# Norm scales broadcast by TensorE, two first output tiles that follow the input, and a last product whose split weights serve both token halves, in a two-layer hybrid trunk

## The chip, the cores and the metric

The kernel runs on one core of a Trainium2 chip. The metric is the device time of one execution in microseconds (us); smaller is better. Three executions of the kernel before the change took 1350.98 to 1352.93 us, with a median of 1351.63 us. One execution was also profiled.

## The reference: what is computed

The input is 512 tokens of 1024 channels in float32. Two layers add to it in place, each followed by a gated feed-forward part, and a norm ends it:

```python
def rms_norm(x, w, eps=NORM_EPS):
    y = x * lax.rsqrt(jnp.mean(x * x, axis=-1, keepdims=True) + eps)
    return y * w
...
x = x + pool_attention_mixer(rms_norm(x, norm_mix[0]), ...)   # pooling + windowed attention
x = x + conv_ffn(rms_norm(x, norm_ffn[0]), ...)
x = x + ssd_mixer(rms_norm(x, norm_mix[1]), ...)              # Mamba-2, with a norm of its own
x = x + conv_ffn(rms_norm(x, norm_ffn[1]), ...)
return rms_norm(x, norm_final)
...
def conv_ffn(h, w_up, conv_w, conv_b, w_down):
    hid = causal_dwconv(h @ w_up, conv_w, conv_b)             # 1024 -> 2 x 2816
    u, g = jnp.split(hid, 2, axis=-1)
    return (jax.nn.silu(g) * u) @ w_down                      # 2816 -> 1024
```

So there are six norms. Each needs, for every token, one number over all 1024 (in the Mamba part 2048) channels: the reciprocal root of a mean square.

## The kernel before

**Layout.** Channels lie on the 128 partitions and tokens along the free dimension, so `x` is eight tiles of 128 x 512. A product takes weights of 128 x 128 as the stationary operand and 512 tokens as the moving one. Each float32 operand is split into a high and a low part of type float32r, and `gemm` (L143 to L148) issues three matmuls for each pair: high by high (L146), high by low (L147), low by high (L148). Weights come in tiles of 128 x 1024 by DMAs on SyncE's queue (SP); ScalarE (ACT) rounds the high part (L138) and VectorE (DVE) subtracts it for the low part (L139). The buffers `w`, `wh` and `wl` have three copies each.

**A norm.** The norm's weights are multiplied into the activations when they are split (L151, L152). The scale of each token is applied only behind the next product, since it is the same for all channels: `scaled` (L232) multiplies the product in PSUM by `rb`, the 512 scales repeated on all 128 partitions. `Stat` makes them. ACT squares each tile of `x` (L171), GpSimd (POOL) adds the squares up (L172), TensorE sums over partitions with a column of ones (L179), and a chain of seven small operations (L183 to L189) makes a reciprocal root `rt` with tokens on the partitions (128 x 4). To lie along the free dimension on all partitions, `rt` goes by one DMA to `flat` in DRAM (L192) and by a second one back from there to `rb`, repeated 128 times (L194). Both are in SP's queue, in order with the loads of weights. The product does not wait for the scale, but its results stay in PSUM until `rb` is there, and PSUM has four buffers `mm`.

**The places by time** (us in the profiled execution): the first projection and pooling mixer (0 to 165, the attention in it from 74 on), the first feed-forward part (165 to 515), the Mamba part (515 to 990; it applies its `rb` at L232 for the projections, and that of its inner norm at L226, behind the product with `ssm_w_out`), and the second feed-forward part (990 to the end). The step sizes of the Mamba part (`sd`, L527) need `rt` itself, not `rb`.

**The start.** One output tile's weights, t0, are loaded behind the first tile of `x`; its products follow the input tile by tile. The tiles t1 and t2 follow as whole products. Two matmuls on constant data (`WARMUP`) stand ahead of them.

**The end.** `finish_out` (L242 to L262) does the last third of the last down product in two halves of 256 tokens, so that the output of the first half is written while the second is multiplied. Each half loads and splits the same eight weight tiles. The scale of the first half goes through `flat` and `rb`; that of the second half is broadcast by TensorE into PSUM (L198), `rt` repeated as the stationary operand by a unit matrix. Then DVE multiplies each tile by weight and scale (L260) and SP writes it (L262).

**The order of the work** on each engine is not the order of the source. A scheduler sorts the instructions by a simulated timeline ahead of time; each engine then runs its list in order and waits where an operand is missing.

Of the kernel before, what the change touches and what calls it, by code (L numbers as in the profile page):

```python
# [20 lines left out]
P = 128  # L21
T = 512
# [33 lines left out]
K_ROT = K_PH + 3  # L56
NCON = K_ROT + P

WARMUP = 2
INV2PI = 1.0 / (2.0 * math.pi)  # L60
MAGIC = 12582912.0
PI_C1 = 6.28125
# [6 lines left out]
def trunk_kernel(ctx: ExitStack, tc: tile.TileContext, io):  # L69
# [19 lines left out]
    def ct(dt=F32):  # L89
        return sp.tile([P, T], dt, tag="C", name=nm("c"), bufs=16)  # L90
# [4 lines left out]
    def t2(tag, bufs, dt=F32):  # L95
        return tp.tile([P, T], dt, tag=tag, name=nm(tag), bufs=bufs)
# [16 lines left out]
    nc.sync.dma_start(x[:, 0, :], io["xT"][:, 0, :])  # L113

    idle = t2("sq", 2)
    G.memset(idle[:], 1.0)
    A.activation(idle[:, 0:1], idle[:, 1:2], AF.Copy)
# [8 lines left out]
    def pc(c):  # L126
        return par[:, c : c + 1]


    def load_split(src, kt=8, cols=P, eng=None):  # L130
# [3 lines left out]
        nc.sync.dma_start(w[:, :kt, :cols], src)  # L134
        if eng is V:
            V.tensor_copy(h[:, :kt, :cols], w[:, :kt, :cols])
        else:
            A.activation(h[:, :kt, :cols], w[:, :kt, :cols], AF.Copy)  # L138
        V.tensor_tensor(out=l[:, :kt, :cols], in0=w[:, :kt, :cols],  # L139
                        in1=h[:, :kt, :cols].bitcast(F32), op=ALU.subtract)  # L140
        return h, l

    def gemm(ps, ws, kt, rh, rl, first=True, last=True, ts=slice(0, T)):  # L143
        h, l = ws
        for k in range(kt):
            PE.matmul(ps, lhsT=h[:, k, :], rhs=rh[k][:, ts], start=first and k == 0, stop=False)  # L146
            PE.matmul(ps, lhsT=h[:, k, :], rhs=rl[k][:, ts], start=False, stop=False)  # L147
            PE.matmul(ps, lhsT=l[:, k, :], rhs=rh[k][:, ts], start=False, stop=last and k == kt - 1)  # L148
# [7 lines left out]
    class Stat:  # L156
# [17 lines left out]
        def finish(self, dim, eps, copy=True):  # L174
# [14 lines left out]
            V.tensor_tensor(out=r, in0=r, in1=q, op=ALU.mult)  # L189
            if copy:  # L190
                flat = dp.tile([NB, P], F32, tag="flat", name=nm("flat"), bufs=2)
                nc.sync.dma_start(flat[:nb, :].rearrange("c p -> p c"), r)  # L192
                rb = t2("rb", 1)
                nc.sync.dma_start(rb[:, :w], flat[:nb, :].rearrange("c p -> (c p)").partition_broadcast(P))  # L194
                return rb, r
            pb = aux()
            for c in range(nb):
                PE.matmul(pb[:, c * P : (c + 1) * P], lhsT=r[:, c : c + 1].to_broadcast([P, P]), rhs=ident,  # L198
# [43 lines left out]
    def finish_out(down, nj, kh, kl):  # L242
        H = T // 2
        warm = tp.tile([P, 1], F32, tag="warm", name="warm", bufs=1)
        A.activation(warm[:], ones[:, 0:1], AF.Sqrt)
        scale = []
        for half in range(2):
            ts = slice(half * H, (half + 1) * H)
            stat = Stat(KD, H, late=2)
            for n in range(KD):  # L250
                ws = load_split(down[n], nj)
                ps = mm()
                gemm(ps[:, :H], ws, nj, kh, kl, ts=ts)
                V.tensor_tensor(out=x[:, n, ts], in0=ps[:, :H], in1=x[:, n, ts], op=ALU.add)
                stat.add(x[:, n, ts])
            scale.append(stat.finish(D, EPS, copy=half == 0)[0])
        for half in range(2):
            ts = slice(half * H, (half + 1) * H)
            for k in range(KD):
                V.scalar_tensor_tensor(out=x[:, k, ts], in0=x[:, k, ts], scalar=pc(C_NFIN + k),  # L260
                                       in1=scale[half][:, :H], op0=ALU.mult, op1=ALU.mult)
                nc.sync.dma_start(io["out"][k * P : (k + 1) * P, ts], x[:, k, ts])  # L262


    def ffn(layer, cur, nxt):
# [68 lines left out]
        return res  # L334


    def mixer(cur, nxt, first_ws):
        poolw = tp.tile([P, 4, P], F32, tag="R", name="poolw", bufs=3)
        nc.sync.dma_start(poolw[:], io["poolw"])
        rb, rt = cur.stat.finish(D, EPS)  # L340
        hp, lp, ha, la = bt(), bt(), bt(), bt()

        def project(t):
            ws = first_ws[t] if t < len(first_ws) else load_split(io["wmi"][t])
            ps = mm()
            gemm(ps[:], ws, KD, cur.hs, cur.ls)
            return ps


# [396 lines left out]
```

## Time and profile before

| | |
|---|---|
| median of three runs | 1351.63 us (1350.98 to 1352.93) |
| the profiled execution's own time | 1350.57 us |
| its span, from the first to the last instruction | 1348.8 us |
| TensorE busy (modelled ends) | 1294.2 us, 96% |
| DVE, ACT, POOL busy | 877.4, 594.7 and 183.8 us |
| share of the chain that ended last | PE 83%, DMA 7%, DVE 4%, ACT 2%, issue 2%, POOL 1% |
| mean granted clock of TensorE | 0.986 |

A row of the timeline reads: start, length (both us), engine, line, operation, output and inputs, and in brackets how long the engine had been idle before and on what. In a row of waits stand the waiting engine and line, what it waited for, the total, the number of times and the longest. A row of windows has, behind the stretch and its length, the busy time and the number of instructions of PE, of its weight loads (PEld), of DVE, ACT and POOL, then the mean granted clock, the share of the DMA engines in use and GB/s.

### The profile page before, as it was taken

To read this page: it belongs to the slowest core of one execution; us is meant where nothing else is said; L and a number is where in the kernel's file an instruction comes from. 1 tells how busy PE (TensorE), PEld (TensorE's weight loads), DVE (VectorE), ACT (ScalarE), POOL (GpSimd) and SP (SyncE) were. 2 spreads that over 40 slices of the span, in tenths; PEclk is the share of its full clock that TensorE was granted. 3 is DMA by queue.
4 is the path that set the end of the run, shared out by engine and by line. 5 is a ranking of instruction groups with operands and counts; after the bars stand their busy time and mean duration, and the time that the engine had idled before them with its cause. 6 is when DMAs were issued, how large, how long until landed. Compare 5 with 4: busy or idle time off the path is not lost.

```text
span 1348.8 us, 16284 instructions
## 1 busy us (share of the span) xinstructions
PE 1294.2 (96%) x6242; PEld 1055.9 (78%) x6242; DVE 877.4 (65%) x1348; ACT 594.7 (44%) x813; POOL 183.8 (14%) x167
## 2 busy tenths in 40 slices
PE   7898999999999999899999999988999999999995
PEld 5665878888888887778888888777878888888895
DVE  6664568457647764687888878844577467557764
ACT  6273445234324444465556655532344234324451
POOL 4552300000000012021222122212000000000021
PEclk9989999999999999999999999998999999999998
DMA  6411233333233323343333333213233332333352
GB/s 231 135 33 47 94 86 102 102 103 97 78 114 96 101 89 95 91 122 109 100 105 105 114 95 105 84 63 89 91 97 92 105 105 88 99 96 106 97 157 82
DMA packets 46574, 134.81 MB, mean 100 GB/s; under 512 B 8288, under 2 KB 10720, under 8 KB 46496
## 3 DMA queue, kind: packets, MB, share of 16 engines
q1 hardware_dynamic: 45856, 132.46, 31.9%
q0 software_dynamic: 640, 1.31, 0.4%
q8 instruction: 49, 0.80, 0.2%
q14 instruction: 29, 0.24, 0.1%
HBM read 129.74 MB, written 2.17 MB: 98 GB/s over the span
## 4 chain that ended last, share of the span: by engine, by line
PE 83%; DMA 7%; DVE 4%; ACT 2%; issue 2%; POOL 1%; SPq 0%; DVEq 0%; ACTq 0%; POOLq 0%
PE mm L146 26%; PE mm L148 26%; PE mm L147 25%; DMA flat<-rt 3%; DMA rb<-flat 2%; PE yp L621 1%; DVE wl L139 1%; PE yp L624 1%; DMA R<-scr 1%; ACT wh L138 1%; PE ax L627 1%; PE mm L412 1%; PE yp L447 1%; DVE c L238 1%; PE ax L451 1%
## 5 line engine op out<-in xcount | busy, mean ns | idle before, releaser
L146 PE MATMUL mm<-a,wh 128*128 128x512 f32 x1232 | 485.3, 394 | 13.0 <-DVE p L226 7.5
L147 PE MATMUL mm<-a,wh 128*128 128x512 f32 x1232 | 484.3, 393 | 5.3 <-DVE a L152 5.3
L148 PE MATMUL mm<-a,wl 128*128 128x512 f32 x1232 | 485.6, 394 | 2.3 <-DVE wl L139 2.3
L138 ACT ACTIVATE wh<-w 128x1024 fp32r<-128x1024 f32 (+1 forms) x225 | 233.5, 1042 | 422.0 <-PE mm L147 371.0
L139 DVE TENSOR_TENSOR wl<-w,wh 128x1024 fp32r<-128x1024 f32 (+1 forms) x226 | 285.9, 1268 | 84.3 <-ACT wh L138 83.2
L146 PEld LDWEIGHTS mm<-a,wh 128*128 128x128 f32 x1232 | 232.7, 189 | 64.3 <-issue 13.5
L147 PEld LDWEIGHTS mm<-a,wh 128*128 128x128 f32 x1232 | 232.8, 189 | 57.7 <-DVE a L152 9.3
L148 PEld LDWEIGHTS mm<-a,wl 128*128 128x128 f32 x1232 | 232.6, 189 | 53.7 <-DVE wl L139 4.4
L172 POOL TENSOR_TENSOR sacc<-sacc,sq 128x512 f32<-128x512 f32 (+1 forms) x53 | 81.4, 1535 | 897.4 <-ACT sq L171 896.1
L232 DVE TENSOR_TENSOR p<-mm,rb 128x512 f32<-128x512 f32 x120 | 82.4, 689 | 98.6 <-PE mm L148 78.0
L238 DVE SCALAR_TENSOR_TENSOR acc<-p,par,acc 128x511 f32<-128x511 f32 (+1 forms) x176 | 131.1, 748 | 3.1 <-ACT acc L236 0.3
L148 PE MATMUL mm<-b,wl 128*128 128x512 f32 (+1 forms) x304 | 104.5, 348 | 5.3 <-DVE wl L139 5.3
L147 PE MATMUL mm<-b,wh 128*128 128x512 f32 (+1 forms) x304 | 105.4, 348 | 0.0
L146 PE MATMUL mm<-b,wh 128*128 128x512 f32 (+1 forms) x304 | 103.8, 348 | 1.0 <-ACT wh L138 1.0
L229 DVE TENSOR_TENSOR x<-mm,x 128x512 f32<-128x512 f32 x56 | 37.9, 690 | 100.8 <-PE mm L148 100.8
L147 PE MATMUL mm<-c,wh 128*128 128x512 f32 x240 | 93.3, 390 | 0.0
L146 PE MATMUL mm<-c,wh 128*128 128x512 f32 x240 | 92.3, 391 | 0.7 <-ACT c L151 0.7
L148 PE MATMUL mm<-c,wl 128*128 128x512 f32 x240 | 92.6, 389 | 0.0
L236 ACT ACTIVATE acc<-p,par 128x512 f32<-128x512 f32 x88 | 71.1, 810 | 32.1 <-DVE p L232 31.7
L238 DVE SCALAR_TENSOR_TENSOR c<-p,par,c 128x511 f32<-128x511 f32 (+2 forms) x96 | 75.3, 784 | 1.9 <-ACT c L236 0.7
L148 PEld LDWEIGHTS mm<-b,wl 128*128 128x128 f32 x304 | 58.2, 192 | 12.5 <-DVE wl L139 5.5
L146 PEld LDWEIGHTS mm<-b,wh 128*128 128x128 f32 x304 | 58.1, 192 | 9.0 <-ACT wh L138 1.4
(172 smaller groups left out, 1137.1 us busy)
## 6 DMA issues: line engine op xcount, KB each, us to landing
w<-wup SPq DMA_DIRECT2D x88, 512.0 KB, 3.5
w<-wsi SPq DMA_DIRECT2D x48, 512.0 KB, 3.5
w<-wdn SPq DMA_DIRECT2D x32, 448.0 KB, 3.3
w<-wdn SPq DMA_DIRECT2D x24, 512.0 KB, 3.5
R<-scr SPq DMA_DIRECT2D x32, 256.0 KB, 3.6
w<-wso SPq DMA_DIRECT2D x16, 512.0 KB, 3.7
w<-wmi SPq DMA_DIRECT2D x10, 512.0 KB, 5.6
w<-wmo SPq DMA_DIRECT2D x8, 512.0 KB, 3.6
```

Source lines behind the costliest of these rows:

```text
L138: A.activation(h[:, :kt, :cols], w[:, :kt, :cols], AF.Copy)
L139: V.tensor_tensor(out=l[:, :kt, :cols], in0=w[:, :kt, :cols], in1=h[:, :kt, :cols].bitcast(F32), op=ALU.subtract)
L146: PE.matmul(ps, lhsT=h[:, k, :], rhs=rh[k][:, ts], start=first and k == 0, stop=False)
L147: PE.matmul(ps, lhsT=h[:, k, :], rhs=rl[k][:, ts], start=False, stop=False)
L148: PE.matmul(ps, lhsT=l[:, k, :], rhs=rh[k][:, ts], start=False, stop=last and k == kt - 1)
L172: self.lanes[lane].tensor_tensor(out=acc[:, :w], in0=acc[:, :w], in1=sq[:, :w], op=ALU.add)
L229: V.tensor_tensor(out=x[:, n, :], in0=ps[:], in1=x[:, n, :], op=ALU.add)
L232: V.tensor_tensor(out=out, in0=ps, in1=rb[:], op=ALU.mult)
L236: A.activation(dst, src, AF.Identity, scale=pc(taps[-1]), bias=pc(b))
L238: V.scalar_tensor_tensor(out=dst[:, s:], in0=src[:, : T - s], scalar=pc(taps[-1 - s]), in1=dst[:, s:], op0=ALU.mult, op1=ALU.add)
L412: PE.matmul(ss[p][:, j, k0:], lhsT=q[2 * jj + j][rows, n * P : (n + 1) * P], rhs=k[rows, keys], start=True, stop=True)
L447: PE.transpose(pt[:, h // 4, (h % 4) * P : (h % 4 + 1) * P], sms[h][:, c0 : c0 + P], ident)
```

## The change

1. **The scales.** `finish` no longer sends `rt` through DRAM. It broadcasts by TensorE at every norm: four matmuls of 128 x 128 in float32 into a PSUM buffer `aux`, and ACT copies the result to `rb`. The reciprocal root takes six small operations in place of seven. Only the last half of the last norm is used from PSUM directly, as before.
2. **The start.** The products of t0 and t1 both follow the input: for each tile of `x`, three matmuls of each. Their weights are loaded and split in halves of four channel tiles, t0's high part by DVE and t1's by ACT. The squares stand behind all the splits in the source. `WARMUP` is 3, and the constant data for it come from DVE in place of POOL.
3. **The end.** The eight down tiles are loaded once and split once, in halves, into 32 tiles of 128 x 512 taken from the pools `A` and `C`, and serve both halves of the tokens. For the second half ACT multiplies `x` by the weights ahead of the scale, and DVE multiplies by the scale in four operations of 128 x 2 x 256, each followed by a write of 256 KB. `late`, the number of tiles whose squares bypass POOL, is 1 in place of 2.
4. **The scheduler** sorts everything anew.

```diff
@@ finish @@
-            V.tensor_tensor(out=q, in0=r, in1=r, op=ALU.mult)
+            V.scalar_tensor_tensor(out=q, in0=r, scalar=-0.5, in1=r, op0=ALU.mult, op1=ALU.mult)
             V.tensor_tensor(out=q, in0=q, in1=v, op=ALU.mult)
-            V.tensor_scalar(q, q, -0.5, 1.5, op0=ALU.mult, op1=ALU.add)
-            V.tensor_tensor(out=r, in0=r, in1=q, op=ALU.mult)
-            if copy:
-                flat = dp.tile([NB, P], F32, tag="flat", name=nm("flat"), bufs=2)
-                nc.sync.dma_start(flat[:nb, :].rearrange("c p -> p c"), r)
-                rb = t2("rb", 1)
-                nc.sync.dma_start(rb[:, :w], flat[:nb, :].rearrange("c p -> (c p)").partition_broadcast(P))
-                return rb, r
+            V.scalar_tensor_tensor(out=r, in0=q, scalar=1.5, in1=r, op0=ALU.add, op1=ALU.mult)
             pb = aux()
             for c in range(nb):
                 PE.matmul(pb[:, c * P : (c + 1) * P], lhsT=r[:, c : c + 1].to_broadcast([P, P]), rhs=ident,
...
@@ finish_out @@
-        scale = []
-        for half in range(2):
-            ts = slice(half * H, (half + 1) * H)
-            stat = Stat(KD, H, late=2)
+        ws = []
+        for n in range(KD):
+            w = wp.tile([P, 8, P], F32, tag="w", name=nm("w"), bufs=3)
+            nc.sync.dma_start(w[:, :nj, :], down[n])
+            hl = []
+            for q in range(2):
+                h, l = ((ct(F32R) if n >= KD // 2 else at()).rearrange("p (k m) -> p k m", k=4) for _ in range(2))
+                wq = w[:, 4 * q : 4 * q + 4, :]
+                A.activation(h, wq, AF.Copy)
+                V.tensor_tensor(out=l, in0=wq, in1=h.bitcast(F32), op=ALU.subtract)
+                hl.append((h, l))
+            ws.append(hl)
+        def run(ts):
+            w = ts.stop - ts.start
+            stat = Stat(KD, w, late=1)
             for n in range(KD):
-                ws = load_split(down[n], nj)
                 ps = mm()
-                gemm(ps[:, :H], ws, nj, kh, kl, ts=ts)
+                for q in range(2):
+                    gemm(ps[:, :w], ws[n][q], 4, kh[4 * q :], kl[4 * q :], first=q == 0, last=q == 1, ts=ts)
...
+        rb, _ = run(body).finish(D, EPS)
+        stat = run(rest)
...
+        for k in range(KD):
+            A.activation(os[k // 4][:, k % 4, :], x[:, k, rest], AF.Copy, scale=pc(C_NFIN + k))
+        pb, _ = stat.finish(D, EPS, copy=False)
+        for k in range(0, KD, 2):
+            o = os[k // 4][:, k % 4 : k % 4 + 2, :]
+            V.tensor_tensor(out=o, in0=o, in1=pb[:, :H].unsqueeze(1).to_broadcast([P, 2, H]), op=ALU.mult)
+            nc.sync.dma_start(out[:, k : k + 2, rest], o)
...
@@ start @@
-    first_ws = [load_split(io["wmi"][0], eng=V)]
-    for k in range(1, KD):
-        nc.sync.dma_start(x[:, k, :], io["xT"][:, k, :])
     for k in range(KD):
+        if k:
+            nc.sync.dma_start(x[:, k, :], io["xT"][:, k, :])
+        if k in (0, 1, 3, 4):
+            i = (0, 1, 3, 4).index(k)
+            t, ks = i % 2, slice(4 * (i // 2), 4 * (i // 2) + 4)
+            nc.sync.dma_start(raw[t][:, ks, :], io["wmi"][t][:, ks, :])
+    for k in range(KD):
+        if k % 4 == 0:
...
         st[0].split(k)
-    first_ws += [load_split(io["wmi"][t]) for t in (1, 2)]
+        for t in range(2):
+            gemm(first_ps[t][:], [w[:, k : k + 1, :] for w in halves[t]], 1, st[0].hs[k:], st[0].ls[k:],
+                 first=k == 0, last=k == KD - 1)
```

How the scheduler's lists move is shown at three places.

**SP at the start.** `x` is the input, `wmi` the weights of the first projection; `w_84` is t0's tile before, `w_89` and `w_92` are those of t0 and t1 after. Before:

```order
L113 DMA x<-xT 128x512
L134 DMA w_84<-wmi 128x1024
L663 DMA x<-xT 128x512 x7
L134 DMA w_129<-wmi 128x1024
L134 DMA w_135<-wmi 128x1024
```

After:

```order
L113 DMA x<-xT 128x512
L690 DMA w_89<-wmi 128x512
L686 DMA x<-xT 128x512
L690 DMA w_92<-wmi 128x512
L686 DMA x<-xT 128x512 x2
L690 DMA w_89<-wmi 128x512
L686 DMA x<-xT 128x512
L690 DMA w_92<-wmi 128x512
L686 DMA x<-xT 128x512 x3
```

Ahead of the last input tile stand now two weight tiles in halves, where there was one; no third weight tile stands directly behind them.

**PE at the inner norm of the Mamba part.** Before, the sums over partitions (`ax<-con,sacc`) stand among the products, with no other instruction of the norm after them on PE; `c` and `a` are split activations:

```order
L147 MATMUL mm_6738<-c_6735,wh_6770 128x512
L148 MATMUL mm_6738<-c_6734,wl_6771 128x512
L179 MATMUL ax_6799<-con,sacc_4203 128x1 x4
L147 MATMUL mm_6825<-c_6735,wh_6857 128x512
L148 MATMUL mm_6825<-c_6734,wl_6858 128x512
L146 MATMUL mm_6896<-c_6734,wh_6928 128x512
```

After, the sums are there as well, and 38 matmuls of 128 x 512 behind them comes the broadcast (`ax<-con,rt`), in the middle of another product:

```order
L145 MATMUL mm_6984<-c_6729,wh_7016 128x512
L146 MATMUL mm_6984<-c_6730,wh_7016 128x512
L147 MATMUL mm_6984<-c_6729,wl_7017 128x512
L190 MATMUL ax_6826<-con,rt_6819 128x128 x4
L145 MATMUL mm_6984<-c_6733,wh_7016 128x512
L146 MATMUL mm_6984<-c_6734,wh_7016 128x512
```

The broadcast waits for `rt` in PE's list, and everything behind it waits with it. At the other norms it stands 42 (first mixer), 30 (first feed-forward), 29 (Mamba projection) and 30 (second feed-forward) such matmuls behind the sums.

**SP at the end of the program.** `wdn` are the weights of the last product, `out` the result. Before:

```order
L134 DMA w_9978<-wdn 128x1024
L134 DMA w_10013<-wdn 128x1024
L134 DMA w_10048<-wdn 128x1024
L192 DMA flat_9835<-rt_9827 128x2x1
L194 DMA rb_9837<-flat_9835 128x256
L134 DMA w_10082<-wdn 128x1024
L262 DMA out<-x 128x256 x16
```

After:

```order
L242 DMA w_9612<-wdn 128x1024
L242 DMA w_9622<-wdn 128x1024
L242 DMA w_9632<-wdn 128x1024
L269 DMA out<-x 128x256 x8
L278 DMA out<-o_10135 128x2x256 x2
L278 DMA out<-o_10136 128x2x256 x2
```

The load of the last weight tile stood behind both transfers of the scale; now no load stands behind a transfer that waits for a scale.

More of the change, by code (lines that the diff above doesn't have):

```diff
@@ L57 @@
 NCON = K_ROT + P
-WARMUP = 2
+WARMUP = 3
 INV2PI = 1.0 / (2.0 * math.pi)
@@ L115, in trunk_kernel @@
     idle = t2("sq", 2)
-    G.memset(idle[:], 1.0)
-    A.activation(idle[:, 0:1], idle[:, 1:2], AF.Copy)
+    V.memset(idle[:], 1.0)
+    first = tp.tile([P, 1], F32, tag="first", name="first", bufs=1)
+    V.memset(first[:], 1.0)
+    A.activation(first[:], first[:], AF.Copy)
     ips = aux()
@@ L250, in finish_out @@
+        def run(ts):
+            w = ts.stop - ts.start
+            stat = Stat(KD, w, late=1)
             for n in range(KD):
-                ws = load_split(down[n], nj)
                 ps = mm()
-                gemm(ps[:, :H], ws, nj, kh, kl, ts=ts)
-                V.tensor_tensor(out=x[:, n, ts], in0=ps[:, :H], in1=x[:, n, ts], op=ALU.add)
+                for q in range(2):
+                    gemm(ps[:, :w], ws[n][q], 4, kh[4 * q :], kl[4 * q :], first=q == 0, last=q == 1, ts=ts)
+                V.tensor_tensor(out=x[:, n, ts], in0=ps[:, :w], in1=x[:, n, ts], op=ALU.add)
@@ L255, in finish_out @@
                 stat.add(x[:, n, ts])
[L256 to L262, printed above, removed]
+            return stat
@@ new lines, in finish_out @@
+        body, rest = slice(0, H), slice(H, T)
+        rb, _ = run(body).finish(D, EPS)
+        stat = run(rest)
+        for k in range(KD):
+            V.scalar_tensor_tensor(out=x[:, k, body], in0=x[:, k, body], scalar=pc(C_NFIN + k),
+                                   in1=rb[:, :H], op0=ALU.mult, op1=ALU.mult)
+            nc.sync.dma_start(io["out"][k * P : (k + 1) * P, body], x[:, k, body])
+        os = [tp.tile([P, 4, H], F32, tag="X", name=nm("o"), bufs=2) for _ in range(2)]
+        for k in range(KD):
+            A.activation(os[k // 4][:, k % 4, :], x[:, k, rest], AF.Copy, scale=pc(C_NFIN + k))
@@ L265, in ffn @@
+        pb, _ = stat.finish(D, EPS, copy=False)
+        out = io["out"].rearrange("(k p) t -> p k t", p=P)
+        for k in range(0, KD, 2):
+            o = os[k // 4][:, k % 4 : k % 4 + 2, :]
+            V.tensor_tensor(out=o, in0=o, in1=pb[:, :H].unsqueeze(1).to_broadcast([P, 2, H]), op=ALU.mult)
+            nc.sync.dma_start(out[:, k : k + 2, rest], o)
     def ffn(layer, cur, nxt):
@@ L334, in rope_tables, with mixer @@
         return res
-    def mixer(cur, nxt, first_ws):
+    def mixer(cur, nxt, first_ps):
         poolw = tp.tile([P, 4, P], F32, tag="R", name="poolw", bufs=3)
@@ L343, in project @@
         def project(t):
[L344 removed]
+            if t < len(first_ps):
+                return first_ps[t]
             ps = mm()
[L346 removed]
+            gemm(ps[:], load_split(io["wmi"][t]), KD, cur.hs, cur.ls)
             return ps
@@ L659, in ssm @@
             nxt.tile(n)
-    first_ws = [load_split(io["wmi"][0], eng=V)]
-    for k in range(1, KD):
-        nc.sync.dma_start(x[:, k, :], io["xT"][:, k, :])
     st = [Next(C_NMIX), Next(C_NFFN), Next(C_NMIX + 8), Next(C_NFFN + 8)]
+    raw, halves, first_ps = [], [], [mm(), mm()]
+    for t in range(2):
+        raw.append(wp.tile([P, 8, P], F32, tag="w", name=nm("w"), bufs=3))
+        halves.append([wp.tile([P, 8, P], F32R, tag=tag, name=nm(tag), bufs=3) for tag in ("wh", "wl")])
     for k in range(KD):
+        if k:
[4 more added lines that the diff above has]
+            nc.sync.dma_start(raw[t][:, ks, :], io["wmi"][t][:, ks, :])
+    for k in range(KD):
+        if k % 4 == 0:
+            ks = slice(k, k + 4)
+            for t in range(2):
+                (h, l), w = halves[t], raw[t]
+                if t:
+                    A.activation(h[:, ks, :], w[:, ks, :], AF.Copy)
+                else:
+                    V.tensor_copy(h[:, ks, :], w[:, ks, :])
+                V.tensor_tensor(out=l[:, ks, :], in0=w[:, ks, :], in1=h[:, ks, :].bitcast(F32), op=ALU.subtract)
         st[0].split(k)
-    first_ws += [load_split(io["wmi"][t]) for t in (1, 2)]
+        for t in range(2):
+            gemm(first_ps[t][:], [w[:, k : k + 1, :] for w in halves[t]], 1, st[0].hs[k:], st[0].ls[k:],
+                 first=k == 0, last=k == KD - 1)
     for k in range(KD):
@@ L672, in trunk_kernel @@
     nc.sync.dma_start(row[:], io["row"].partition_broadcast(P))
-    mixer(st[0], st[1], first_ws)
+    mixer(st[0], st[1], first_ps)
     ffn(0, st[1], st[2])
```

7 lines of the change are left out of this document (2 added, 5 removed).

## The prediction

> **What bounds the kernel now.** I read the page's busy shares first, then the windows by place, then TensorE's waits, then the tile `rb`, then the timeline around each wait. The busy shares:
>
> ```profile
> PE 1294.2 (96%) x6242; PEld 1055.9 (78%) x6242; DVE 877.4 (65%) x1348; ACT 594.7 (44%) x813; POOL 183.8 (14%) x167
> ```
>
> TensorE (PE) is busy nearly all the time, so only its gaps, and the matmuls that it runs at a low clock behind a gap, can be won. The windows say where they are (PE busy and its instructions come first, the granted clock stands behind POOL's count):
>
> ```profile
> 0.00:30.00 30.00, 22.18 (x72) 13.94 (x73) 19.32 (x17) 20.04 (x29) 14.98 (x16) 0.94 0.62 221
> 30.00:75.00 45.00, 38.82 (x166) 29.05 (x164) 28.55 (x51) 13.02 (x20) 22.97 (x28) 0.89 0.48 139
> ...
> 165.00:195.00 30.00, 27.93 (x128) 22.95 (x127) 13.80 (x23) 10.95 (x13) 0.00 (x0) 1.00 0.24 62
> 195.00:515.00 320.00, 320.00 (x1413) 265.00 (x1412) 204.68 (x255) 124.56 (x156) 8.67 (x5) 1.00 0.32 98
> 515.00:600.00 85.00, 78.83 (x402) 61.55 (x402) 53.23 (x109) 44.46 (x58) 9.89 (x7) 1.00 0.38 106
> 600.00:840.00 240.00, 240.00 (x1351) 197.22 (x1350) 199.71 (x360) 139.81 (x179) 56.99 (x35) 1.00 0.35 106
> 840.00:960.00 120.00, 109.65 (x508) 87.55 (x509) 72.83 (x105) 49.87 (x68) 21.32 (x14) 0.94 0.26 80
> 960.00:990.00 30.00, 27.25 (x124) 22.35 (x123) 10.45 (x19) 7.72 (x11) 1.53 (x1) 1.00 0.28 78
> ...
> 1290.00:1349.00 59.00, 43.71 (x340) 42.83 (x340) 29.35 (x56) 19.83 (x32) 11.79 (x10) 0.90 0.43 128
> ```
>
> Inside a feed-forward part (195 to 515) and inside the scan (600 to 840) PE has no gap. A matmul of 128 x 512 takes 320.00/1413 = 0.226 us there. The gaps lie at the start, at the end, and where a norm has just been computed: 30 to 75, 165 to 195, 515 to 600, 840 to 960, 960 to 990. What PE waited for:
>
> ```profile
> PE mm L148 <- DVE wl L139: 7.5, 6, 5.3
> PE mm L146 <- DVE p L226: 7.5, 1, 7.5
> ...
> PE mm L146 <- DVE p L232: 4.8, 2, 2.7
> ...
> PE ax L530 <- DVE sd L527: 2.5, 1, 2.5
> ...
> PE mm L146 <- ACT wh L138: 1.0, 2, 0.6
> ```
>
> L226 and L232 are the multiplications by `rb`, which empty PSUM. PE ran out of free `mm` buffers. What these multiplications waited for is in the view of the tile `rb` (us, times):
>
> ```profile
>   DMA rb<-flat: 56.1, 6
> ```
>
> All six trips of a scale through DRAM made DVE wait, 9.4 us each; the four `mm` buffers hide a part of it. That trip is what the change removes.
>
> **Price of the new broadcast.** Its four matmuls are in float32, 128 x 128. Two like it, warm and one behind the other, and the two that the kernel already has at its end, cold (each counts as two instructions there):
>
> ```profile
> 556.63 0.39 PE L531 MATMUL ax<-sd,con 128*128 128x128 f32 x2
> 556.85 0.39 PE L532 MATMUL ax<-con,sd 128*128 128x128 f32 x2
> ```
>
> ```profile
> L198 PE MATMUL ax<-con,rt 128*128 128x128 f32 x4 | 1.2, 455 | 1.6 <-DVE rt L189 1.6
> ```
>
> Warm, 556.85 - 556.63 = 0.22 us each, so 0.9 for four; cold, 1.2 for two, so 2.4. The broadcasts stand among running matmuls, so I take the warm end, and 1.0 with the change of operand. Five full norms cost PE 5.0 us, the half norm 0.5. ACT's copy to `rb` lies beside PE. The sixth small operation that is saved (0.2 us) is off the path everywhere but at the very end.
>
> **The inner norm of the Mamba part.** The sums, the finished `rt`, and PE's gap:
>
> ```profile
> 894.54 0.95 PE L179 MATMUL ax<-con,sacc 128*128 128x1 f32 x8
> ```
>
> ```profile
> 900.82 0.17 DVE L189 TENSOR_TENSOR rt<-rt 128x4 f32<-128x4 f32 x1
> ```
>
> ```profile
> 915.20 0.76 PE L146 MATMUL mm<-a,wh 128*128 128x512 f32 x1 [7.52 <-DVE p L226]
> ...
> 920.45 0.52 PE L146 MATMUL mm<-a,wh 128*128 128x512 f32 x1
> ```
>
> `rt` is complete at 901.0, 5.5 us behind the sums (895.5). The broadcast stands 38 matmuls behind them: 38 x 0.226 = 8.6 us, so at 904.1 PE finds `rt` ready and does not wait. `rb` follows 1.0 + about 0.7 (ACT) later, at 905.8, and the first L226 ends near 906.5. PE came to its gap at 915.20 - 7.52 = 907.7. So the whole 7.5 goes. Between the two quoted starts lie twelve matmuls in 5.25 us, at half rate: 5.25 - 12 x 0.226 = 2.5 us go too. Less 1.0 for the broadcast: **9.0 us** (6.5 if rows of ACT or DVE delay `rb` by 2.5; 9.5 at best).
>
> The half rate is the clock gate of the Trainium skill, "TensorE: Matmul & The Clock Gate", Part 1: behind an idle window TensorE runs at half its clock until it has been busy for some 3.4 us. The rows show half rate for 5.25 us; by the page's figure alone the cold part would be an estimated 1.7 us, and the gain here 8.2; the rows decide.
>
> **The feed-forward parts.** The row L232 has two waits, 4.8 in all, the longer 2.7; the windows 165 to 195 and 960 to 990 have gaps of 2.07 and 2.75. Here the broadcast stands 30 matmuls, 6.8 us, behind the sums, more than the 5.5 of the chain above. Gains 2.1 - 1.0 = **1.1** and 2.7 - 1.0 = **1.7** (each between 0 and that).
>
> **Entry of the Mamba part.** The window 515 to 600 has 85.00 - 78.83 = 6.2 us of gaps, 2.5 of them in L530, whose operand `sd` needs `rt` and a long chain of DVE operations in which the loads' subtractions and `rb`'s multiplications are interleaved. The broadcast costs 1.0. Gaps that hang on DVE's pile-up behind `rb` go, a little remains: 6.2 - 0.7 - 1.0 = **4.5** (2.0 if L530 and the first scan operands still wait; 5.2 at best).
>
> **Start and mixer, to the attention.** DVE, and PE:
>
> ```profile
> 45.60 0.69 DVE L327 TENSOR_TENSOR L<-L,rb 128x512 f32<-128x512 f32 x1 [9.57 <-DMA rb<-flat]
> ...
> 65.53 0.68 DVE L232 TENSOR_TENSOR c<-mm,rb 128x512 f32<-128x512 f32 x1
> ```
>
> ```profile
> 60.25 0.39 PE L148 MATMUL mm<-a,wl 128*128 128x512 f32 x1
> ...
> 71.17 2.05 PE L381 MATMUL ax<-c,poolw 128*128 128x512 f32 x2 [2.26 <-DVE c L378]
> ...
> 74.00 2.28 PE L412 MATMUL mm<-c,c 64*128 64x256 f32 x14
> ```
>
> The projections end at 60.5; from there PE has little but waits until 74.0. The rotary tables (L327) and the pooling wait for `rb` at 45.6, and DVE comes to the last pooling tile only at 65.53. The start:
>
> ```profile
> 7.79 12.53 POOL L172 TENSOR_TENSOR sacc<-sacc,sq 128x512 f32<-128x512 f32 x7 [6.53 <-ACT sq L171]
> ...
> 16.87 2.31 DVE L139 TENSOR_TENSOR wl<-w,wh 128x1024 fp32r<-128x1024 f32 x1
> ...
> 26.44 0.39 PE L146 MATMUL mm<-a,wh 128*128 128x512 f32 x1
> 27.80 0.95 PE L179 MATMUL ax<-con,sacc 128*128 128x1 f32 x8
> ```
>
> ```profile
> L139 DVE TENSOR_TENSOR wl<-w,wh 128x1024 fp32r<-128x1024 f32 (+1 forms) x226 | 285.9, 1268 | 84.3 <-ACT wh L138 83.2
> ```
>
> PE idles 7.8 of its first 30 us, since t0 alone needs 3 matmuls for an input tile; t2 begins at 26.44. With t0 and t1 behind the input there are six, and t1 (24 matmuls, 5.4 us) is done in gaps. But the last split of the input comes no sooner: DVE has t1's low half as well, and beside POOL's additions it is slow (2.31 us at 16.87, against 1268 ns on average). Between 0 and 2.6 earlier, I take 1.8. Then the sums fall at 26.0, the broadcast 42 matmuls (9.5 us) behind their end at 36.5, and `rb` at 38.2, 7.4 us ahead of 45.6. The projections end at 60.5 - 1.8 + 1.0 = 59.7, and DVE takes the last pooling tile at once, at 60.1. From there to the attention it was 74.00 - 65.53 = 8.5 us, of which about 1.0 was the low clock at 71.17 (window: 0.89). So 67.6: **6.4 us** earlier (4.4 if the pooling's chain through POOL stays behind; 7.4 if `rb` alone decided).
>
> **The end.** SP, ACT, PE and DVE:
>
> ```profile
> 1320.01 0.38 SPq L134 DMA_DIRECT2D w<-wdn  x1
> ```
>
> ```profile
> 1325.76 1.06 ACT L138 ACTIVATE wh<-w 128x1024 fp32r<-128x1024 f32 x1 [6.18 <-DMA w<-wdn]
> ```
>
> ```profile
> 1326.93 0.58 PE L148 MATMUL mm<-b,wl 128*128 128x256 f32 x1 [5.26 <-DVE wl L139]
> 1327.31 0.41 PE L146 MATMUL mm<-b,wh 128*128 128x256 f32 x1
> ...
> 1330.30 0.29 PE L148 MATMUL mm<-b,wl 128*128 128x256 f32 x1
> ```
>
> ```profile
> 1341.88 3.22 DVE L260 SCALAR_TENSOR_TENSOR x<-x,par,ax 128x256 f32<-128x256 f32 x8 [1.38 <-PE ax L198]
> ```
>
> The last weight tile was issued at 1320.01, behind both trips of the first half's scale, and PE stood for 5.26 us. Now all eight tiles are there before the second half begins. 5.3 goes, with the half rate behind it (sixteen matmuls; the fourteen steps from 1327.31 to 1330.30 take 0.21 us each, where half of 0.226 would do: 16 x 0.1 = 1.5) and the 1.0 of L146 on `wh`. Against it: 0.5 for the broadcast, and the first pass, which now has to take all its splits (sixteen half subtractions, 8 x 1.27 = 10.1 us of DVE) beside the last convolutions, and a `w` buffer of three; 0 to 4 us, I take 1.5. **5.8.** Behind the last product: four multiplications of 512 columns cost 4 x 0.69 = 2.8 us by L327's row (PSUM operand unlike it) against 3.22, the small operation 0.2 and a tile fewer in the sums 0.3; against that the last write is twice as large, for which I take 0.5 between 0 and 1.5. **0.4** (from -0.6 to 1.0).
>
> **Sum.** 6.4 + 1.1 + 4.5 + 9.0 + 1.7 + 5.8 + 0.4 = 28.9 us. The profiled execution took 1350.57 (span 1348.8 and 1.8 around it), so 1321.7; it was 1.1 below the median of its runs, so the median becomes **1322.7 us**.
>
> **Rivals.**
> *The start gives nothing and the pooling keeps its pace.* DVE's two-input operations take turns with POOL's seven additions (the row at 16.87 speaks for it), so t0 and t1 end no sooner than t2 began, 1.8 lost, and the pooling's own chain through POOL and DVE sets the attention's start, 2.6 lost: 1322.7 + 4.4 = 1327.1. The Trainium skill, "SBUF — State Buffer", on the two sides of SBUF, has this as an exclusive lock: a DVE operation with two SBUF inputs and a GpSimd operation that reads SBUF block each other for a whole instruction. Against it, the squares now stand behind the splits. Chance 0.12.
> *The first pass of the last product waits for its splits.* All eight tiles must pass DVE beside the last gate; PE then stands about as long as it did at 1326.93, 5.3: 1328.0. Against it: PE's new list puts 84 matmuls of 0.11 us, 9.5 us for four tiles, ahead of the first that needs the last gated tile, and four tiles are 4 x 1.27 = 5.1 us of DVE. Chance 0.10.
> *PE waits at each broadcast.* PE is in order; if DVE and ACT finish `rt` 2 us behind the broadcast's place at five norms, 10 us come back: 1332.7. Against it: 5.5 us of chain and 6.6 to 9.5 of distance. Chance 0.05.
> *Slower.* In the scan, 600 to 840, PE never waits, with eight groups of 30 us, but the order is new there and DVE is busy 199.71 of 240. The loads that the scan needs:
>
> ```profile
> R<-scr SPq DMA_DIRECT2D x32, 256.0 KB, 3.6
> ```
>
> If one of them in each group is now issued too late and PE stands its 3.6 us and then runs 2.5 cold, 8 x 6.1 = 48.8 us: 1371.5. It decides from (28.9 + 2.7)/8 = 4.0 us a group; before, none showed. Chance 0.03.
> *The scales' trips matter less than the waits say* (another wait stands right behind each): gain within 2.7 us of none. Chance 0.02.
>
> **How the numbers follow.** The forecast has 0.68. Its bounds together (all at the best 33, all at the worst 15) give some 5 us below and 9 above, unlikely all at once; the range takes in the first three rivals: 1315.0 to 1333.0. About 0.2% (2.7 us) is what a measurement of this kernel can tell from no change. Faster: 0.68 + 0.12 + 0.10 + 0.05 = 0.95, same 0.02, slower 0.03.
>
> **What would show it.** In the profile after: no row of `flat`; in the waits of PE no L226 or L232 row over 1 us; `ax<-con,rt` with idle time under 0.5 us and 0.9 to 1.1 us for four; the attention's first matmul of 64 x 256 near 67.6; the last down product without a gap over 2 us, and its last matmul near 1308.3 (1336.8 less 28.5). It is wrong if PE waits at the broadcasts, if the scan shows gaps, or if the waits move to the pooling and to the splits of the last product.

## The result, and the profile after

The changed kernel takes 1318.59 us (median of 4 runs, 1317.97 to 1319.26), the kernel before 1352.15 us (the three runs above and a fourth, 1350.98 to 1352.93): a ratio of 0.9753, 95% interval 0.9736 to 0.9769, a gain of 33.6 us where 28.9 was forecast. The profiled execution has a span of 1316.4 us, against 1348.8: 32.4 us less.

The page of the changed kernel, busy shares and chain:

```profile
PE 1288.6 (98%) x6280; PEld 1056.2 (80%) x6280; DVE 869.1 (66%) x1342; ACT 596.7 (45%) x829; POOL 179.7 (14%) x168
...
PE 94%; DVE 2%; DMA 1%; issue 1%; ACT 1%; POOL 1%; SPq 0%; DVEq 0%; ACTq 0%; POOLq 0%
```

The DMA share of the chain went from 7% to 1%. TensorE's windows after (borders moved by what has been gained):

```profile
0.00:30.00 30.00, 24.26 (x86) 15.86 (x87) 22.64 (x30) 20.63 (x31) 13.44 (x15) 1.00 0.74 247
30.00:75.00 45.00, 40.11 (x188) 31.45 (x187) 31.62 (x70) 18.34 (x38) 21.30 (x27) 0.96 0.38 115
...
160.00:190.00 30.00, 30.00 (x142) 25.12 (x141) 19.49 (x30) 15.30 (x19) 0.00 (x0) 1.00 0.30 89
...
500.00:590.00 90.00, 90.00 (x462) 72.46 (x461) 57.27 (x119) 50.91 (x67) 13.42 (x8) 1.00 0.35 104
590.00:830.00 240.00, 240.00 (x1351) 197.24 (x1350) 200.77 (x359) 140.63 (x180) 58.82 (x35) 1.00 0.34 107
830.00:940.00 110.00, 106.50 (x513) 86.22 (x512) 72.75 (x100) 49.09 (x67) 22.05 (x14) 0.98 0.27 86
940.00:970.00 30.00, 30.00 (x141) 25.08 (x141) 17.32 (x27) 13.73 (x18) 1.52 (x1) 1.00 0.27 89
```

The gaps behind the norms at 165, 515 and 960 are gone, and the one in 840 to 960 has shrunk from 10.4 to 3.5 us. The scan (590 to 830) is as full as it was. TensorE's waits after, the whole list down to 1.2 us:

```profile
PE mm L146 <- DVE a L151: 5.6, 3, 2.7
PE ax L468 <- ACT pT L466: 3.8, 4, 1.2
PE ax L398 <- DVE c L395: 3.6, 1, 3.6
PE ax L122 <- DVE first L118: 1.5, 1, 1.5
PE ax L190 <- DVE rt L187: 1.4, 1, 1.4
PE mm L429 <- DVE st L435: 1.3, 1, 1.3
PE mm L145 <- DVE x L259: 1.2, 1, 1.2
```

No row of a multiplication by `rb` is left. The only broadcast with a wait is the last one of the program (1.4), which always had it (1.6 before). In the tile `rb` the old waits for a DMA (56.1 us, six times) have become waits for ACT's copy:

```profile
  ACT rb L195: 13.1, 5
```

By place, taken from the starts of the same sums over partitions in both profiles, the gain of 32.4 us is:

| stretch | before, us | after, us | gain | forecast |
|---|---|---|---|---|
| start to the attention's scores (64 x 256) | 74.00 | 68.76 | 5.2 | 6.4 |
| to the sums of the first feed-forward part | 93.47 | 94.15 | -0.7 | 0 |
| to the sums of the Mamba part | 363.36 | 361.94 | 1.4 | 1.1 |
| entry and scan, to the inner norm's sums | 363.71 | 357.60 | 6.1 | 4.5 |
| to the sums of the second feed-forward part | 75.47 | 65.99 | 9.5 | 9.0 |
| to the last matmul of the last product | 366.77 | 357.48 | 9.3 | 7.5 |
| behind it | 12.02 | 10.48 | 1.5 | 0.4 |

The table says where the time went, not which of the three edits brought it. That was the question for the experiments. By the forecast the scales bring what lies behind the norms, the new start about 2, the new last product about 6. The rival: the scales bring it all, since the other gaps were made by the same trips through DRAM.

### The profile page after: what moved, and what is told of

Its sections match the earlier page's. It is cut to its first block, busy times and chain, and to the rows that moved or that the text cites. A ratio compares the mean times of both kernels' runs of the same rounds, so it can differ in the third digit from the quotient of the medians.

```text
span 1316.4 us, 16329 instructions
## 1 busy us (share of the span) xinstructions
PE 1288.6 (98%) x6280; PEld 1056.2 (80%) x6280; DVE 869.1 (66%) x1342; ACT 596.7 (45%) x829; POOL 179.7 (14%) x168
## 4 chain that ended last, share of the span: by engine, by line
PE 94%; DVE 2%; DMA 1%; issue 1%; ACT 1%; POOL 1%; SPq 0%; DVEq 0%; ACTq 0%; POOLq 0%
PE mm L147 29%; PE mm L146 29%; PE mm L145 29%; PE yp L638 1%; PE ax L644 1%; PE yp L641 1%; PE mm L429 1%; PE yp L464 1%; DMA w<-wdn 1%; PE ax L468 1%; PE ax L603 1%; PE ax L612 0%; DVE a L151 0%; PE ax L190 0%; PE ax L178 0%
## 5 line engine op out<-in xcount | busy, mean ns | idle before, releaser
L137 ACT ACTIVATE wh<-w 128x1024 fp32r<-128x1024 f32 (+1 forms) x208 | 215.8, 1041 | 420.2 <-PE mm L146 373.8
L138 DVE TENSOR_TENSOR wl<-w,wh 128x1024 fp32r<-128x1024 f32 (+1 forms) x208 | 262.4, 1264 | 77.2 <-ACT wh L137 75.8
L224 DVE TENSOR_TENSOR p<-mm,rb 128x512 f32<-128x512 f32 x120 | 82.3, 689 | 91.6 <-PE mm L147 84.2
L146 PE MATMUL mm<-b,wh 128*128 128x512 f32 x176 | 68.7, 392 | 0.0
L147 PE MATMUL mm<-b,wl 128*128 128x512 f32 x176 | 67.7, 389 | 0.0
L145 PE MATMUL mm<-b,wh 128*128 128x512 f32 x176 | 67.0, 390 | 0.0
L634 POOL TENSOR_TENSOR R<-R,c 128x512 f32<-128x512 f32 x24 | 37.6, 1580 | 195.3 <-ACT R L633 135.3
L311 ACT ACTIVATE acc<-acc 128x512 f32<-128x512 f32 x44 | 27.8, 632 | 79.1 <-DVE acc L230 79.0
```

The costliest lines, as they stand in the source:

```text
L224: V.tensor_tensor(out=out, in0=ps, in1=rb[:], op=ALU.mult)
L311: A.activation(g[:], g[:], AF.Silu)
L634: G.tensor_tensor(out=R[:], in0=R[:], in1=Ct[:, cs].unsqueeze(1).to_broadcast([P, 4, P]), op=ALU.mult)
```

## The experiments

The experiments ran in three groups of four, each on a chip of its own, and the kernel before was run again with each: its medians were 1362.60 us with experiments 1 to 4, 1352.92 with 5 to 8 and 1358.08 with 9 to 12. The spread is itself a finding, below: the kernel before, which makes the trips, differs by 10 us from group to group, the kernels with broadcasts by less than 3. So ratios are against the kernel before on the same chip, and the broadcast kernels are also compared by their own times.

**1. The broadcasts alone.** The edit is the first hunk of the change's diff, made in the kernel before.

> The kernel before with the scales' broadcast by TensorE alone; start and end are as before. By the forecast's terms: mixer 4.6 (6.4 less 1.8 of the start), feed-forward parts 1.1 and 1.7, Mamba entry 4.5, inner norm 9.0, together 20.9 us; and since no load stands behind a trip in SyncE's queue any more, the stall of 5.3 us in the last product and its 1.5 of half rate should go as well, less 0.5 for the half broadcast: 27 us, about 1325. Rival, that another wait stands close behind each trip: under 15 us gained, 1337 or more. Rival, that TensorE waits at the broadcasts: idle time at them over 1 us each.

Measured: 1319.24 us, ratio 0.9688 (0.9669 to 0.9708). That is 6 us below the 1325 expected, and within 0.7 us of the whole change. Its profile has the same span within 0.8 us, and in the last product none of the 5.3 us stall; what TensorE still waits for there:

```profile
PE ax L191 <- DVE rt L188: 1.4, 1, 1.4
PE mm L146 <- ACT wh L138: 1.0, 2, 0.6
...
PE ax L179 <- ACT X L167: 0.6, 1, 0.6
```

The last matmul of the last product comes at 1306.14, in the whole change at 1305.92. So the scales bring nearly all of it: the stall that the forecast wrote to the new last product goes with the trip, as the expectation of this experiment already had it.

**2. The new start alone.**

> The kernel before with the new start alone. If the mixer hangs on rb, and rb on the sums over partitions, the sums come about 2.6 to 4 us sooner and the attention 2 to 3 us sooner: 1349 to 1350. Rival, the turns of VectorE and GpSimd and the pooling's own chain hold the attention back: the sums sooner, the attention not, 1352 (no change).

Measured: 1367.48 us, ratio 1.0043 (1.0027 to 1.0058): 4.9 us slower. The sums come sooner (25.33 against 26.42 in the kernel of experiment 3, with the old start on the same chip), but the attention starts at 77.42 against 74.01. Neither theory had a loss. TensorE's waits up to 74 us and behind:

```profile
PE mm L415 <- DVE c L364: 4.2, 1, 4.2
```

```profile
PE mm L148 <- DVE p L234: 4.6, 1, 4.6
PE mm L415 <- DVE st L421: 3.3, 2, 2.0
```

`rb` came no sooner, as DVE's timeline shows:

```profile
46.07 0.69 DVE L329 TENSOR_TENSOR L<-L,rb 128x512 f32<-128x512 f32 x1 [11.19 <-DMA rb<-flat]
...
76.07 0.75 DVE L154 SCALAR_TENSOR_TENSOR b<-ax,par,b 128x512 fp32r<-128x512 f32 x1 [2.95 <-ACT b L153]
76.74 0.34 DVE L421 CUSTOM_DVE_ANT_0 c<-mm,con,row 128x128 f32<-128x128 f32 x1
```

In experiment 3 the wait for `rb` ended at 45.00: here `rt` was sent off no sooner (31.9 us, there 31.7), and the trip took longer. So TensorE runs out of work earlier and stands longer (4.2 us, where it stood 3.1 at the same place in experiment 3); and the scheduler has put the softmax's reads of the scores (L421) behind another operation that waits 2.95 us for ACT, so TensorE waits for the `mm` buffers of the scores. In the window 68 to 78 the granted clock is 0.50, against 0.65 with the old start. How the loss divides among these was not separated.

**3. The new last product alone.**

> The kernel before with the new last product alone; the scale of the first half still goes through DRAM, but with no load behind it. Theory: the stall of 5.3 goes, with 1.5 of half rate and 1.0 of waits for weights, and 1.5 behind the last matmul: 9 us, about 1343. Rival, that the splits of eight tiles ahead of the first half cost TensorE time: 4 to 5 us gained, 1347.5.

Measured: 1360.05 us, ratio 0.9975 (0.9962 to 0.9988): 2.6 us gained, not 9. Loads no longer stand behind the trip, and yet TensorE stands, now for an addition that frees PSUM. TensorE's wait, and DVE's timeline:

```profile
PE mm L146 <- DVE x L267: 6.7, 2, 5.7
```

```profile
1322.47 0.42 DVE L267 TENSOR_TENSOR x<-mm,x 128x256 f32<-128x256 f32 x1
1336.65 2.46 DVE L275 SCALAR_TENSOR_TENSOR x<-x,par,rb 128x256 f32<-128x256 f32 x6 [13.76 <-DMA rb<-flat]
1339.03 0.42 DVE L267 TENSOR_TENSOR x<-mm,x 128x256 f32<-128x256 f32 x1
```

DVE has the first half's multiplications ahead of the second half's additions and stands 13.8 us before them. The wait changed its place, not its size: with the old end on the same chip (experiment 2) the longest wait there was 6.2 us, here it is 5.7.

**4. The change without the broadcasts.**

> The changed kernel with the scales sent through DRAM again; start and end are the new ones. Theory: it keeps the gain of the start (2 to 3) and of the end (9), and loses the rest: 1340 to 1341. Rival, that the parts hang together (the new start gives nothing without an early rb): 1343 or more.

Measured: 1366.71 us, ratio 1.0023 (1.0009 to 1.0038), slower than before. The parts hang together, more than the rival had it, which foresaw no loss: without an early `rb` the new start and last product are worth less than nothing.

**5. Broadcasts and new start; 6. broadcasts and new last product.**

> The kernel before with the broadcasts and the new start; the end is the old one. What the profiles of the changed kernel and of the broadcasts alone show: the sums over partitions come 2.6 us sooner with the new start, the last pooling tile 1.3, the attention 0.1. So theory: 0 to 0.7 us beside the broadcasts alone (1319.24), 1318.5 to 1319.3. Rival, by the forecast: 1.8 to 2.6 sooner, 1317.

> The kernel before with the broadcasts and the new last product; the start is the old one. Theory: the stall of the last product was the trip's, and has gone with it; what the kept weights add is the 1.0 of two waits for weights less the 1.2 of one wait for a PSUM buffer, and 0.6 behind the last matmul: 1318.5. Rival, by the forecast: 5.8 and 0.4 belong to the new last product, and 1313 comes out.

Measured: 1321.44 us (1320.71 to 1322.36), ratio 0.9768 (0.9755 to 0.9782), with the start; 1319.14 us (1317.95 to 1319.98), ratio 0.9750 (0.9737 to 0.9764), with the last product. Beside 1319.24 for the broadcasts alone, the new last product brings 0.1. The kernel with the new start lies 2.2 above it, outside both values of its expectation. That the start costs this of itself is not shown: of the five runs of the broadcasts alone, two had a mean granted clock of 0.993 and took 1321.09 and 1321.53, the other three had 0.995 and 0.996 and took at most 1319.24, while all four runs with the new start had 0.990 to 0.993. And beside experiment 6 the changed kernel, which has the new start as well, is 0.5 us faster. With the new last product the tail behind the last matmul is 11.1 us against 11.1 with the old one. With the new start the attention begins at 68.04, 0.8 sooner than with the broadcasts alone, but the next sums come at 165.97, 3.7 later. The windows of the kernel with the new start show the low clock (behind POOL):

```profile
58.00:68.00 10.00, 5.15 (x23) 2.56 (x20) 5.51 (x13) 3.09 (x8) 3.74 (x4) 0.68 0.16 53
68.00:85.00 17.00, 16.88 (x62) 12.38 (x63) 12.87 (x72) 12.99 (x50) 6.51 (x16) 0.70 0.00 0
```

In the changed kernel the second of these windows has 1.00 and 74 matmuls. By the clock records of the traces TensorE ran at half rate from 61.7 to 71.9 us and again from 78.7 to 85.6 with the new start, in the changed kernel from 64.7 to 68.2 alone. So the start's earlier work meets the same wait for the pooling, and more of what follows runs at half rate. I read that as a matter of when the gap falls; it led to experiment 9.

**7. The price of a broadcast.** The edit, in `finish`:

```diff
-            for c in range(nb):
+            for c in [c for c in range(nb) for _ in range(2 if copy else 1)]:
```

> The changed kernel with each of the broadcast's matmuls issued twice at the six places where the result is copied to rb (22 more float32 matmuls of 128 x 128, to the same values). By the forecast's price of 0.22 us each, all on TensorE's path except at the mixer: 18 x 0.22 = 4.0 us more, about 1322.6. If they lie beside other work: under 1 us more. If they run at the low clock: 8 us more.

Measured: 1322.37 us, 3.8 more than the changed kernel. The stretches of the table show it one by one: 362.83 in place of 361.94, 358.54 in place of 357.60, 66.88 in place of 65.99. Each four matmuls cost 0.9 us, 0.22 each; at the mixer they are hidden. The forecast's price holds.

**8. The pooling on VectorE.**

```diff
-                G.tensor_copy(dst[:, :sh], src[:, :sh])
-                G.tensor_tensor(out=dst[:, sh:], in0=src[:, sh:], in1=src[:, : T - sh], op=ALU.add)
+                V.tensor_copy(dst[:, :sh], src[:, :sh])
+                V.tensor_tensor(out=dst[:, sh:], in0=src[:, sh:], in1=src[:, : T - sh], op=ALU.add)
```

> The changed kernel with the additions of the pooling on VectorE in place of GpSimd. If GpSimd's two steps of the second pooling tile (59.79 to 63.59, 3.8 us) set the attention's start, TensorE's wait of 3.6 shrinks to about 1.6, since VectorE takes some 0.9 for each step: 1316.5. Rival, that VectorE's own list is the bound there: 1318.6 or more.

Measured: 1321.57 us, ratio 0.9768 (0.9754 to 0.9781), some 3 us worse. TensorE's wait for the pooling fell only from 3.6 to 3.0, and the attention began at 69.36, where it was 68.76 in the changed kernel; the clock was 0.70 from 68 to 85 here too. So the rival holds: DVE's list is as much a bound as POOL. How much of the 3 us is the clock alone was not separated.

**9. TensorE kept busy in its wait; 10. the first squares on VectorE; 11. both.** The edits, in `pool` and at the start:

```diff
+            po = aux()
+            for _ in range(3 if g == 1 else 0):
+                PE.matmul(po[:], lhsT=poolw[:, g, :], rhs=ub[:], start=True, stop=True)
...
-            po = aux()
...
-    st = [Next(C_NMIX), Next(C_NFFN), ...
+    st = [Next(C_NMIX, lanes=(V,)), Next(C_NFFN), ...
```

> The changed kernel with three more matmuls on the second pooling tile, whose result is overwritten, put where TensorE waits 3.6 us for the pooling. Nothing else gets faster by them. If the low clock behind that wait costs (the pooling's matmuls at 2.0 for two, the transposes at 1.06 for four, and in some runs the scores too), 1 to 3 us are gained and the runs lie closer together: 1316.5, granted clock 0.997 or more. Rival, that the clock there costs nothing or the added matmuls push the rest back: 1318.6 to 1321.

> The changed kernel with the first norm's squares added up by VectorE in place of GpSimd. If the turns with GpSimd make VectorE's splits slow (1.40 to 1.77 us for a half subtraction, 0.68 without), the splits of the input end 2 to 3 us sooner although VectorE has seven additions more, and the sums over partitions come at 20.5 to 21.5 in place of 23.8. If the mixer follows: 1316. Rival, that VectorE is then the bound by its own work: sums at 23.8 or later, and no gain.

> Both of the two edits above: the first norm's squares on VectorE, and the three matmuls in TensorE's wait. Theory: the two gains add up, 1314 to 1315. Rival, that the attention's start hangs on the pooling's own chain behind the last projection, which the earlier start moves too: the same as the better of the two.

Measured: 1315.62 us (1315.48 to 1315.80), ratio 0.9690 (0.9671 to 0.9708), with the three matmuls; 1317.61 us (1315.33 to 1319.44), 0.9704 (0.9683 to 0.9725), with the squares; 1312.39 us (1312.27 to 1313.16), 0.9667 (0.9649 to 0.9686), with both. Three matmuls whose result is overwritten gain 3.0 us. The windows of the kernel with them:

```profile
58.00:68.00 10.00, 9.54 (x50) 5.47 (x48) 8.36 (x27) 4.78 (x8) 3.78 (x5) 1.00 0.22 68
68.00:85.00 17.00, 16.62 (x74) 12.26 (x73) 12.00 (x63) 15.54 (x67) 7.91 (x20) 1.00 0.01 1
```

The clock stays at 1.00 (0.84 in 58 to 68 in the changed kernel), and the runs lie within 0.3 us, where those of the changed kernel lie within 1.3. But the clock is not all of it. In the two profiles the gain lies ahead of the sums of the first feed-forward part (159.62 us against 162.92), and the low stretch that went there lasted 3.4 us at half rate, so it can account for 1.7 us at most. With the edit the scheduler also sorted the lists anew. In the changed kernel DVE's reads of the scores (L435) stand behind an operation that waits for ACT:

```profile
67.42 0.75 DVE L151 SCALAR_TENSOR_TENSOR b<-ax,par,b 128x512 fp32r<-128x512 f32 x1 [2.89 <-ACT b L150]
68.08 0.34 DVE L435 CUSTOM_DVE_ANT_0 c<-mm,con,row 128x128 f32<-128x128 f32 x1
```

With the three matmuls they stand ahead of it, and TensorE's wait for them fell from 1.3 to 0.3 us. What the clock and what the order brought was not separated.

By the Trainium skill, "TensorE: Matmul & The Clock Gate", Part 1, the gate watches windows that run freely, so that where a gap falls in them varies from run to run; the narrower spread without the gap agrees with that.

With the squares on VectorE (experiment 10) the sums come at 21.49 in place of 23.84. The same operations on DVE with POOL adding squares beside them (changed kernel):

```profile
9.38 0.74 DVE L151 SCALAR_TENSOR_TENSOR a<-x,par,a 128x512 fp32r<-128x512 f32 x1
10.04 1.52 DVE L699 CAST wh<-w 128x512 fp32r<-128x512 f32 x1
11.60 1.66 DVE L700 TENSOR_TENSOR wl<-w,wh 128x512 fp32r<-128x512 f32 x1
13.18 3.45 DVE L151 SCALAR_TENSOR_TENSOR a<-x,par,a 128x512 fp32r<-128x512 f32 x2
```

and without:

```profile
10.31 0.75 DVE L151 SCALAR_TENSOR_TENSOR a<-x,par,a 128x512 fp32r<-128x512 f32 x1
10.97 0.42 DVE L699 CAST wh<-w 128x512 fp32r<-128x512 f32 x1
11.31 0.68 DVE L171 TENSOR_TENSOR sacc<-sacc,sq 128x512 f32<-128x512 f32 x1
11.91 0.68 DVE L700 TENSOR_TENSOR wl<-w,wh 128x512 fp32r<-128x512 f32 x1
```

1.66 has become 0.68, 1.52 has become 0.42, and DVE does seven additions more in less time. In the changed kernel the slow ones end in step with POOL's additions: 11.56 us behind an end of POOL at 11.28, 13.26 behind 12.71, 14.93 behind 14.38. The lock of the Trainium skill's "SBUF — State Buffer", the two sides of SBUF, is what these rows look like: an operation of DVE waits until the one of POOL has ended. The squares alone bring little (1.0 us, with a wide spread), since the gap before the pooling is still there; with the gap filled they bring 3.2 us more, so that both together gain more than the two gains added up; why was not followed. The kernel with both is 6.2 us below the changed one.

**12. The trip on another queue**, in the kernel before; `finish` issues both transfers from the queue `q_`, where it is given:

```diff
-                nc.sync.dma_start(flat[:nb, :].rearrange("c p -> p c"), r)
+                (q_ or nc.sync).dma_start(flat[:nb, :].rearrange("c p -> p c"), r)
...
-            scale.append(stat.finish(D, EPS, copy=half == 0)[0])
+            scale.append(stat.finish(D, EPS, copy=half == 0, q_=A)[0])
```

> The kernel before with the last norm's two transfers of the first half (rt to DRAM and back to all partitions) issued from ScalarE's queue, so that no load of weights stands behind them; the trip is as long as it was. If the stall of 5.3 us in the last product came from SyncE's order, it goes, with its half rate: 5 to 7 us gained. Rival, that VectorE's list holds it (the multiplications by that scale stand ahead of the last subtraction, and of additions that free PSUM): less than 1.5 us gained, with TensorE waiting on VectorE at the same place.

Measured: 1355.97 us, ratio 0.9986 (0.9974 to 0.9998): 2.1 us gained, between the two theories. TensorE's waits in the last product, and DVE's:

```profile
PE mm L146 <- ACT wh L138: 2.5, 3, 1.5
PE mm L148 <- DVE wl L139: 1.0, 2, 0.8
```

```profile
DVE wl L139 <- ACT wh L138: 12.1, 9, 6.8
```

The second transfer waits for the first one's landing (they are issued at 1320.3 and 1328.3 us), now in ACT's list, and ACT's rounding of the next weights stands behind it: 3.5 us of TensorE's waits, where the profile of the kernel before has 6.3 (5.3 and 1.0). Behind SP it held a load, behind ACT it holds a split, with DVE (experiment 3) it held the PSUM buffers. In these three kernels the order of the lists decides whom the trip stops, the trip that it stops somebody.

## Why the prediction was right, and where it was not

**The bound** was read rightly: gaps behind norms, made by the trip of the scale, full product stretches that no edit could touch. Without trips the gaps are gone, and the broadcasts alone give 0.9688 (experiment 1).

**The price of the broadcasts**, 0.22 us a matmul and 1.0 a norm, is what experiment 7 measured (0.9). TensorE did not wait at any of the five: their distance from the sums suffices. The rival of waits at the broadcasts fell, and so did the one in the scan: 240.00 of 240 us busy, as before.

**The inner norm** (9.0, measured 9.5) and **the feed-forward parts** (1.1 and 1.4) came as worked out, with the half rate behind the gap counted in; the second feed-forward part, from its sums to the first matmul of the last product, gained 2.1 where 1.7 was forecast. The traces' clock records agree with the rows behind the inner norm's gap: before the change the clock was at half from 910.5 to 920.7 us, of which 5.5 us lie behind the gap.

**The entry of the Mamba part** was mis-sized: 4.5 against 6.1. The window 500 to 590 is completely busy, so the 0.7 that was left standing and the range's 2.0 were too careful; no wait of `sd` remains. That makes 5.2; where the other 0.9 comes from is not settled.

**The end** is the step that failed in its reason. "Now all eight tiles are there before the second half begins" was to free 5.3 us; experiments 1, 3 and 6 show that the broadcast freed them, that the new last product without it frees 2.6, and with it 0.1. The cause that I gave was wrong, and that the sum came near all the same was luck: both edits are in the changed kernel, so the stall goes whichever of them it is credited to. I had read that the last load stands behind the trip, and not asked what else stands there: had the load come, DVE's multiplications by the late scale would have stood ahead of the same work. The sum was too low by 1.8, 0.4 of it in the second feed-forward part above and 1.4 in the last product, which gained 7.2 where 5.8 was forecast. Of the 1.5 that I charged for the splits of eight tiles 1.2 came, as the wait on L259: that addition, which frees a PSUM buffer, stands behind a split (L248) in DVE's list:

```profile
1268.41 1.29 DVE L248 TENSOR_TENSOR c<-w,c 128x512 fp32r<-128x512 f32 x2 [0.81 <-ACT c L247]
1269.62 1.41 DVE L259 TENSOR_TENSOR x<-mm,x 128x256 f32<-128x256 f32 x4
```

So the error lies in the other terms; the second half of the tokens alone gained 6.9, and which term was short was not followed. The rival that the splits bind, with a wait of 5.3, fell.

**Behind the last matmul**, 1.5 in place of 0.4: DVE's four multiplications took 2.48 us and not the 2.8 that I took from L327, the last write of 256 KB took little longer than one of 128 KB (3.9 us from DVE's last operation to the end, 3.7 before), and the broadcast ran warm, 0.68 us against 1.20. The last is not the new product's doing: with the broadcasts alone it was 0.68 as well, in experiment 6 it was 1.20. The changed kernel's rows:

```profile
1309.37 0.68 PE L190 MATMUL ax<-con,rt 128*128 128x128 f32 x4 [1.37 <-DVE rt L187]
1310.09 2.48 DVE L277 TENSOR_TENSOR o<-o,ax 128x512 f32<-128x512 f32 x4 [0.87 <-PE ax L190]
```

**Start and mixer** came to 5.2, where 6.4 was forecast, and 0.7 was given back in the attention; where, was not followed. The start did bring the sums 4.0 us forward (23.84 against 27.80, 2.6 against the broadcasts alone), more than the 1.8 taken, and the mixer kept 0.1 of it: 68.76 against 68.82 with the old start. What eats it can be followed: the last pooling tile is 1.3 us ahead (DVE's L224 at 59.04 against 60.35), and then the scores' softmax reads stand behind another operation in DVE's list, 1.25 us of TensorE (L429 on L435 above). So the first rival, which had a chance of 0.12, came half true: the start was worth nothing, the pooling bounds the attention's start. What I held against it, "the squares now stand behind the splits", was wrong: that is their order in the source, but POOL and DVE are separate lists, and POOL's additions ran from 7.4 to 19.5 us, over the splits.

In the range one step was worked out wrong: all terms at their worst give a gain of 15 us, which is 14 above the forecast and not 9; nothing came near it.

In the profile the gain came out 3.5 us above the forecast, by errors of both signs: 1.6 at the entry, 1.8 at the end, 1.1 behind it, 0.5 at the inner norm and 0.3 in the feed-forward part, against 1.9 at the start and the attention. In the median it was 4.1, since this profiled execution lies 0.4 us below its median and not 1.1. The range held it, in part because the errors offset each other.

## What to carry to other kernels

A wait that returns at many places with one cause should be priced as one edit: before crediting a second edit with the stall that it removes, ask whether the first one's cause stands behind that stall too, and run each part alone and all but one. A transfer that waits for another transfer blocks whatever stands behind it in an in-order list; here moving it to another queue moved the stall, and a broadcast on TensorE for 0.9 us ended it. And where a gap on TensorE can't be closed, look at the clock behind it: three matmuls in the gap, with the new order that came with them, were worth 3 us here.

## What the runs showed of the hardware

The trip through DRAM is not one number. In the four groups of runs the kernel before took 1352.15, 1362.60, 1352.92 and 1358.08 us. The first leg, `rt` to `flat` (2 KB), took a median of 7.5 us in the profile of before and 8.9 and 9.3 us in the profiles of experiments 3 and 2, while the 88 loads of 512 KB for the up products took 3.5 to 3.6 us in all of them. DVE's six waits for `rb` came to 56.1 us in the profile of before and to 66.0 and 69.5 in those of experiments 2 and 3. The kernels with broadcasts and without further edits lay between 1318.6 and 1321.4 us in the three groups in which they ran. No profile of the kernel before itself was taken on the other chips.

The low clock is always 0.5 in the clock records of these traces, and but for the last stretch of each, which the program's end cuts off, it lasts 3.41 us or a multiple of it: 6.83, 10.24, 13.65 or 17.07. Behind the same gap of 3.6 us it lasted one such length in the changed kernel and with the broadcasts alone, three with the new start added to them, where two more followed from 78.7 to 85.6 us. So a small shift of the work adds or takes 3.4 us at half rate at a time. Runs of one kernel differ in their granted clock too: 2.3 us lie between the two groups of runs of experiment 1. Two versions that differ by 2 to 3 us in this kernel can differ by that alone.
